# Heads with fewer gate products between them, and a down projection in 512-column steps

## The chip, the cores and the metric

The kernel runs on one core of a Trainium2 chip (trn2). The metric is the device time of one execution in microseconds. The kernel before takes 2524.01 us (median of three runs, 2521.85 to 2524.84).

Engines, as the profile names them: PE is TensorE's matrix multiply and PEld its weight load, DVE is VectorE, ACT is ScalarE, POOL is GpSimd, SP is SyncE, which issues the transfers.

## The reference

Two layers over 512 latent tokens and 256 context tokens of width 1024. Each layer has three token mixers side by side (retention, grouped-query attention, mLSTM), a gated merge, an output projection, and a gated MLP of width 2816 with a convolution of three taps; each sub-layer ends in a layer norm. In the last layer only latent tokens are asked for.

```
pl = split_proj(modulate(x, shift, scale) @ w_in + b_in)        # queries, keys, values, three gates
y_a = softmax(q @ k.T / 8) @ v                                  # 8 heads, 2 key/value groups, keys: context and latents
z = sigmoid(g_r) * (y_r @ w_r) + sigmoid(g_a) * (y_a @ w_a) + sigmoid(g_m) * (y_m @ w_m)
x = layer_norm(alpha * x + gate * (z @ w_out), ln1_g, ln1_b)
u = conv3(modulate(x, ...) @ w_up) + conv_b;   a, g = split(u)
x = layer_norm(alpha * x + gate * ((silu(g) * a) @ w_down), ln2_g, ln2_b)
```

Everything is float32. The kernel forms a product of float32 matrices from three products of a shorter float type: each operand is split into a high and a low part (`h`, `l`), and high x high, low x high and high x low are added up in PSUM.

## The kernel before

Tokens lie in tiles of 128 (`t` 0 to 3 latents, 4 and 5 context). Weights stream in blocks of 512 KB: a transfer into `raw` (five buffers), ACT casts the high part `wh`, DVE subtracts the low part `wl` (two buffers each; `wblock`, lines 308 to 315).

A Python scheduler, `Mixer`, writes PE's order at build time; the orders of the other engines come from the framework. Its foreground is the list of big products. Background generators (mLSTM, retention, attention, layer norms) are stepped between them: after a step, a generator that yields `d` isn't stepped again until foreground and background products worth `d` of the Mixer's own microseconds have been written (`step_bg`). A foreground that needs a background result steps the generators by force until the result is there (`run`).

Attention (`attention`, generator) takes one head of one query tile per step. Step n writes the scores of head n (`score`, tile `psc`: 2 products of 512 columns, 2 of 256, then maximum, exponential, sum, scaling on DVE and ACT), the six transposes of head n-2 (`flip`, tile `pPT`), and after every fourth head the value products (`av`, tile `pAV`). Then it yields 3.5 (line 1018). PSUM has two pools: three banks "g" for big products, five banks "p" for all the rest; `pAV` keeps one of the five for eight heads.

In layer 1 the foreground beside attention is, in this order: 24 gate blocks (24 products of 512 columns each; `fm`, a chance for the background after every 6), the branch products of mLSTM and retention (`merge(0)`, `merge(1)`), those of attention for tiles 0 and 1 (`merge(2)`, needs both tiles), the output projection of tiles 0 and 1, then both again for tiles 2 and 3. When tiles 0 and 1 are through the output projection their layer norm starts as background (`finish`): sums and scaling on DVE and ACT give `xn`, which PE transposes (`ptr`) for the MLP. Before that, one modulation product (`pp`, `pm`) goes through PE. `gate_rows` spreads the gate of the sub-layer over the partitions (`pgr`).

The MLP works in four groups of the hidden width (5, 5, 6 and 6 blocks of 128). Each group is projected up (`fm`), convolved, multiplied with its gate, split into `ah` and `al`, and projected down (`tm`, line 463): the activation tile is the stationary operand, 256 columns of `w_down` move. The first weight block of a quarter `q` of the 1024 columns holds all but the last two k of the group, the second the last two. Two tiles share a bank. When it is complete, `accumulate` (lines 1109 to 1125) multiplies it by the gate row and adds it to X, two operations on DVE. The fourth group of each layer also feeds the layer norm; it isn't touched by the change.

Of the kernel before, what the change touches and what calls it, by code (L numbers as in the profile page):

```python
# [13 lines left out]
OP = mybir.AluOpType  # L14
# [5 lines left out]
DEPTH = 2  # L20
# [4 lines left out]
NF = D_FF // 128  # L25
# [68 lines left out]
def layout(inputs):  # L94
    f = {k: np.asarray(v) for k, v in inputs.items()}
    A = {}
    A["x"] = f["x"].reshape(SEQ, D)
    A["ctx"] = f["ctx"].reshape(CTX, D)
    A["cT"] = np.stack([f["c"].reshape(8, 128).T, f["c_ctx"].reshape(8, 128).T], axis=2)
    w = f["w_mod"].reshape(DEPTH, 2, 4, 128, 24, 256)  # L100
    A["wmod"] = w.transpose(0, 4, 1, 3, 2, 5).reshape(DEPTH, 24, 2, 128, 1024)
    A["bmodT"] = f["b_mod"].reshape(DEPTH, 6, 8, 128).transpose(0, 3, 1, 2).reshape(DEPTH, 128, 48)
    w_in, b_in = f["w_in"], f["b_in"]
    glb = np.zeros((DEPTH, 128), np.float32)
    for dst, src in ((0, O_LI), (32, O_LI + 4), (64, O_LF), (96, O_LF + 4)):
        glb[:, dst:dst + 4] = b_in[:, src:src + 4]
    fm = [w_in[:, :, c:c + 128] for c in FM_COLS]
    A["wfm"] = np.stack([b.reshape(DEPTH, 8, 128, 128).transpose(0, 2, 1, 3).reshape(DEPTH, 128, 1024) for b in fm], 1)
    A["bfm"] = np.stack([glb] + [b_in[:, c:c + 128] for c in FM_COLS], 2)
    A["wtm"] = np.stack([w_in[:, :, c:c + 256].reshape(DEPTH, 2, 4, 128, 256).transpose(0, 1, 3, 2, 4)  # L110
                         .reshape(DEPTH, 2, 128, 1024) for c in TM_COLS], 1)
    vg = np.concatenate([w_in[:, :, TM_COLS[1]:TM_COLS[1] + 256], w_in[:, :, O_LI:O_LI + 16]], 2)
    A["wvg"] = vg.reshape(DEPTH, 8, 128, 272).transpose(0, 2, 1, 3).reshape(DEPTH, 128, 2176)
    A["btm"] = np.stack([b_in[:, c:c + 256] for c in TM_COLS], 1)
    w = np.stack([f["w_br_mlstm"], f["w_br_ret"], f["w_br_att"]], 1).reshape(DEPTH, 3, 4, 128, 4, 256)
    A["wbr"] = w.transpose(0, 1, 4, 3, 2, 5).reshape(DEPTH, 3, 4, 128, 1024)
    w = f["w_out"].reshape(DEPTH, 2, 4, 128, 4, 256)
    A["wout"] = w.transpose(0, 4, 1, 3, 2, 5).reshape(DEPTH, 4, 2, 128, 1024)
    w = f["w_up"].reshape(DEPTH, 8, 128, 2 * NF, 128)
    A["wup"] = w.transpose(0, 3, 2, 1, 4).reshape(DEPTH, 2 * NF, 128, 1024)  # L120
    w = f["w_down"].reshape(DEPTH, NF, 128, 4, 256)
    A["wdn"] = w.transpose(0, 3, 2, 1, 4)
    A["convT"] = np.stack([f["conv_w"][:, i].reshape(DEPTH, 2 * NF, 128).transpose(0, 2, 1) for i in range(3)]
                          + [f["conv_b"].reshape(DEPTH, 2 * NF, 128).transpose(0, 2, 1)], 3).reshape(DEPTH, 128, 8 * NF)
    A["gnT"] = np.concatenate([f["mlstm_gn_g"].reshape(DEPTH, 4, 128).transpose(0, 2, 1),
                               f["ret_gn_g"].reshape(DEPTH, 4, 128).transpose(0, 2, 1)], 2)
    A["qkg"] = np.concatenate([f["attn_qn_g"], f["attn_kn_g"]], 1)
    dl = f["ret_decay_logit"]
    t = np.zeros((DEPTH, 128, 16), np.float32)
    for d in range(2):  # L130
        for j in range(2):
            t[:, :64, 2 * d + j] = dl[:, d, 2 * j, None]
            t[:, 64:, 2 * d + j] = dl[:, d, 2 * j + 1, None]
        for h in range(4):
            t[:, :, 4 + 4 * d + h] = dl[:, d, h, None]
            t[:, 64 * d:64 * d + 64, 12 + h] = dl[:, d, h, None]
    A["dlog"] = t
    for n in ("ln1_g", "ln1_b", "ln2_g", "ln2_b"):
        A[n] = f[n]
    A["cst"] = _constants()  # L140
    return {k: np.ascontiguousarray(v) for k, v in A.items()}
# [62 lines left out]
def _program(es, nc, tc, I, OUT):  # L204
# [258 lines left out]
    def tm(srcs, lhs, tiles, nks, evac, hook=None, w=256):  # L463
        per = 512 // w
        banks = [tiles[i:i + per] for i in range(0, len(tiles), per)]
        gs = [None] * len(banks)
        tot = sum(nks)
        done = 0
        for src, nk in zip(srcs, nks):
            h, l = src() if callable(src) else wblock(src, nk * w)  # L470
            for bi, ts in enumerate(banks):
                if hook:
                    yield from hook(int(done > 0), ts)
                if done == 0:
                    gs[bi] = gt()
                for i, t in enumerate(ts):
                    for k, pi in [(k, pi) for k in range(nk) for pi in (0, 1)] + [(k, 2) for k in range(nk)]:
                        mm(gs[bi][:, w * i:w * i + w], lhs(done + k, t, pi == 1), (l if pi == 2 else h)[:, w * k:w * k + w],
                           start=(done + k == 0 and pi == 0 and i == 0),
                           stop=(done + k == tot - 1 and pi == 2), skip_group_check=True)  # L480
                    yield
                if done + nk == tot:
                    evac(ts, gs[bi][:, :w * len(ts)].rearrange("p (t c) -> p t c", c=w))
            done += nk

    def x_lhs(xh, xl):
# [359 lines left out]
    def attention(l, qtiles, ydir):  # L846
# [137 lines left out]
        for n in range(len(units) + 3):  # L984
# [28 lines left out]
            if n < len(units) and units[n][1] == 7 and units[n][0] != qtiles[-1]:  # L1013
                yield 2.0
                Q[tn] = stack(qn)
                yield 2.0
            else:
                yield 3.5 if n < len(units) and units[n][0] < 4 else 2.8
        M.done.add(f"a{l}")

    def brow(l, i):
# [87 lines left out]
    def accumulate(l, X, xslot, ts, g, q, rows, first, final):  # L1109
        hf, co = divmod(q, 2)  # L1110
        i = 0
        while i < len(ts):
            n = 1
            while i + n < len(ts) and (ts[i + n] >= 4) == (ts[i] >= 4):
                n += 1
            t = ts[i]
            tmp = stg()
            t3 = tmp[:, :256 * n].rearrange("p (t c) -> p t c", c=256)
            V.tensor_tensor(t3, g[:, i:i + n], bc(rows[int(t >= 4)][hf][:, 256 * co:256 * co + 256], 1, n), op=OP.mult)
            xs = X[:, xslot(t):xslot(t) + n, 256 * q:256 * q + 256]  # L1120
            V.scalar_tensor_tensor(xs, xs, ALPHA if first else 1.0, t3, op0=OP.mult, op1=OP.add)
            if final:
                for u in range(t, t + n):
                    V.bn_stats(bst[:, u, 6 * q:6 * q + 6], X[:, xslot(u), 256 * q:256 * q + 256])
            i += n

    LAT, ALL = ((0, 512),), ((0, 512), (512, 768))

    def layer(l, xT, key):
# [301 lines left out]
        for gr, (go, gnum) in enumerate(zip(GOFF, GROUPS)):  # L1431
# [50 lines left out]
            def keep(q, si, src):  # L1482
# [12 lines left out]
                        kept[q, si] = h, m  # L1495
                return kept[q, si]

            for ts in (((0, 1), (2,), (3,)) if final and last else trips if final else (tuple(range(nqt)),)):
                for q in range(4):
                    n0 = gnum - 2  # L1500
# [37 lines left out]
```

## Time and profile before

| | |
|---|---|
| three runs | 2521.85, 2524.84, 2524.01 us |
| the profiled execution | 2534.83 us, span 2533.0 us, mean granted clock 0.985 |
| PE busy | 2435.9 us, 96% of the span |
| DVE busy | 1574.9 us, 62% |
| ACT busy | 1002.7 us, 40% |
| share of the chain that ended last | PE 85%, DVE 7%, DMA 4%, ACT 3% |

The profile is one execution. A product's duration in it is its way through the array, about 281 ns for 256 columns and 393 ns for 512, and neighbours overlap; the pace is read from the step from one start to the next, or from a stretch divided by its count. PEclk is the granted clock of PE: 1.00 is 2.4 GHz, 0.50 is 1.2 GHz. A number in brackets behind a row is how long the engine had been idle before it, with the instruction that ended the wait.

### The profile page before, as it was taken

The numbers are of one execution on the slowest core, as the hardware profiler recorded it, in microseconds if no ns is written. First come the engines' busy times: TensorE is split into PE (matmuls) and PEld (weight loads), VectorE is DVE, ScalarE is ACT, GpSimd is POOL, SyncE is SP. The second block draws the span as 40 slices with busy tenths as digits, with TensorE's granted clock in tenths as the row PEclk, the third lists the DMA queues.
The fourth block names the chain that finished last, engine by engine and source line by source line (L and its number), as shares of the span: only waits on it lengthen the run. The fifth ranks groups of instructions, "written<-read, shape, count | busy, mean of one in ns | idle before, by whom it ended". The sixth has DMA issues, their size and how long they took to land.

```text
span 2533.0 us, 41667 instructions
## 1 busy us (share of the span) xinstructions
PE 2435.9 (96%) x16552; PEld 2155.9 (85%) x16552; DVE 1574.9 (62%) x3308; ACT 1002.7 (40%) x1802; POOL 92.2 (4%) x111
## 2 busy tenths in 40 slices
PE   6999999999899999999999989999999989999998
PEld 4977998888788988999998878779787788988887
DVE  5556465545477885555545773767565877855557
ACT  4433321455433473232313353434254455633332
POOL 1000001000000000000000010000110000000000
PEclk9999999999999999999999999999999998999999
DMA  7253524322554562212121383354434444533232
GB/s 257 90 171 134 167 94 140 111 82 86 175 165 165 193 243 84 74 53 77 53 76 55 125 292 126 99 172 140 161 122 146 135 134 167 176 105 99 83 106 67
DMA packets 147651, 329.21 MB, mean 130 GB/s; under 512 B 15872, under 2 KB 59136, under 8 KB 147456
## 3 DMA queue, kind: packets, MB, share of 16 engines
q1 hardware_dynamic: 147456, 326.54, 39.4%
q8 instruction: 131, 2.15, 0.4%
q14 instruction: 64, 0.52, 0.1%
HBM read 283.49 MB, written 42.99 MB: 129 GB/s over the span
## 4 chain that ended last, share of the span: by engine, by line
PE 85%; DVE 7%; DMA 4%; ACT 3%; issue 1%; POOL 0%; SPq 0%; DVEq 0%; ACTq 0%; POOLq 0%
PE g L214 72%; PE pAV L214 2%; PE psc L214 2%; PE pPT L218 2%; DVE wl L314 2%; DMA raw<-in_wmod_dram 1%; PE pE L214 1%; PE pNf L214 1%; ACT wh L313 1%; PE pp L214 1%; PE pU L214 1%; DMA raw<-in_wtm_dram 1%; PE pO L214 1%; DMA raw<-in_wup_dram 1%; PE pyt L218 0%
## 5 line engine op out<-in xcount | busy, mean ns | idle before, releaser
L214 PE MATMUL g<-xh,wh 128*128 128x512 f32 (+1 forms) x2448 | 827.9, 353 | 11.0 <-ACT xh L1315 4.7
L214 PE MATMUL g<-xl,wh 128*128 128x512 f32 (+1 forms) x2448 | 814.8, 348 | 1.4 <-DVE xl L442 0.8
L314 DVE TENSOR_TENSOR wl<-raw,wh 128x1024 fp32r<-128x1024 f32 (+3 forms) x358 | 411.9, 1151 | 354.5 <-ACT wh L313 270.8
L313 ACT CAST wh<-raw 128x1024 fp32r<-128x1024 f32 (+3 forms) x358 | 355.2, 992 | 644.4 <-PE g L214 575.5
L214 PEld LDWEIGHTS g<-xh,wh 128*128 128x128 f32 x2448 | 466.7, 191 | 80.2 <-issue 10.0
L214 PEld LDWEIGHTS g<-xl,wh 128*128 128x128 f32 x2448 | 468.0, 191 | 57.3 <-DVE xl L1316 1.3
L214 PE MATMUL g<-xh,wl 128*128 128x512 f32 (+1 forms) x2448 | 511.1, 348 | 3.0 <-DVE wl L314 3.0
L214 PEld LDWEIGHTS g<-xh,wl 128*128 128x128 f32 x2448 | 402.4, 191 | 61.1 <-DVE wl L314 3.4
L214 PE MATMUL g<-wh,ah 128*128 128x256 f32 x808 | 207.3, 284 | 3.6 <-ACT ah L1459 3.6
L214 PE MATMUL g<-wh,al 128*128 128x256 f32 x808 | 206.5, 283 | 2.7 <-DVE al L1460 2.7
L214 PE MATMUL g<-wh,xh 128*128 128x256 f32 (+1 forms) x768 | 203.4, 295 | 3.1 <-ACT wh L313 1.7
L214 PE MATMUL g<-wh,xl 128*128 128x256 f32 (+1 forms) x768 | 199.1, 290 | 3.4 <-DVE xl L1377 2.1
L214 PEld LDWEIGHTS g<-wh,ah 128*128 128x128 f32 x808 | 153.9, 190 | 4.9 <-ACT ah L1459 4.2
L214 PEld LDWEIGHTS g<-wh,xh 128*128 128x128 f32 x768 | 150.9, 196 | 8.2 <-issue 3.3
L214 PEld LDWEIGHTS g<-wh,al 128*128 128x128 f32 x808 | 153.9, 190 | 4.1 <-DVE al L1460 3.5
L214 PEld LDWEIGHTS g<-wh,xl 128*128 128x128 f32 x768 | 151.1, 197 | 4.2 <-DVE xl L1377 2.4
L1420 ACT ACTIVATE tc<-g,conv 128x512 f32<-128x512 f32 (+1 forms) x142 | 96.8, 682 | 132.8 <-PE g L214 131.6
L214 PE MATMUL g<-wl,ah 128*128 128x256 f32 x808 | 144.9, 283 | 0.8 <-DVE wl L314 0.8
L1421 DVE SCALAR_TENSOR_TENSOR tc<-g,conv,tc 128x511 f32<-128x511 f32 (+1 forms) x142 | 88.7, 625 | 83.8 <-ACT tc L1420 83.1
L414 POOL TENSOR_TENSOR rstd<-veps,mhalf 128x1 f32<-128x1 f32 (+3 forms) x68 | 71.8, 1057 | 1797.6 <-DVE veps L412 1783.2
L947 ACT ACTIVATE Pe<-psc,mx 128x256 f32<-128x256 f32 (+1 forms) x144 | 80.7, 565 | 142.2 <-DVE mx L942 96.7
L214 PE MATMUL g<-wl,xh 128*128 128x256 f32 (+1 forms) x768 | 129.1, 289 | 0.9 <-DVE wl L314 0.8
(279 smaller groups left out, 3159.0 us busy)
## 6 DMA issues: line engine op xcount, KB each, us to landing
raw<-in_wup_dram SPq DMA_DIRECT2D x108, 512.0 KB, 3.5
raw<-in_wmod_dram SPq DMA_DIRECT2D x96, 512.0 KB, 5.4
raw<-in_wfm_dram SPq DMA_DIRECT2D x80, 512.0 KB, 3.6
raw<-in_wtm_dram SPq DMA_DIRECT2D x32, 512.0 KB, 5.3
raw<-in_wout_dram SPq DMA_DIRECT2D x32, 512.0 KB, 3.6
raw<-in_wbr_dram SPq DMA_DIRECT2D x28, 512.0 KB, 4.3
dr_g<-stg SPq DMA_DIRECT2D x48, 256.0 KB, 2.0
raw<-in_wdn_dram SPq DMA_DIRECT2D x20, 512.0 KB, 3.6
```

Source lines behind the costliest of these rows:

```text
L214: nc.tensor.matmul(out, lhsT, rhs, **kw)
L218: nc.tensor.transpose(out, in_, ident)
L313: S.copy(h[:, :n], raw[:, :n])
L314: V.tensor_tensor(l[:, :n], raw[:, :n], h[:, :n].bitcast(F32), op=OP.subtract)
L414: G.tensor_tensor(r, t, mhalf[:, :n], op=OP.pow)
L947: S.activation(pe[:, a:b], prs[si][:, :b - a], AF.Exp, bias=mx[:, 3:4], scale=0.125, accum_out=sm[:, si:si + 1])
L1420: S.activation(t[:, a:b], g, AF.Identity, bias=conv[:, jj, 3:4], scale=conv[:, jj, 1:2])
L1421: V.scalar_tensor_tensor(t[:, a + 1:b], g[:, :b - a - 1], conv[:, jj, 0:1], t[:, a + 1:b], op0=OP.mult, op1=OP.add)
```

## The change

Two edits.

In layer 1's attention the generator yields 2.6 in place of 3.5 after each of the first 16 steps (the heads of the first two query tiles). With PE's chances of 6 products of 512 columns, that is 12 gate products between two heads in place of 18.

The down projection of the first three groups of each layer goes through a new function, `tm_wide`: 512 columns of `w_down` move per product, for two halves `hf` of the width in place of four quarters. Each tile has a bank of its own, alternately from pool "g" and pool "p" (there named `gx`). Weight blocks hold two k of 512 columns (one k in the last block of a group of 5): 6 blocks per group in place of 8, from a second arrangement of the same weights. `accumulate_wide` does for one tile and 512 columns what `accumulate` did for two tiles and 256.

```
+    w = f["w_down"].reshape(DEPTH, NF, 128, 2, 512)
+    A["wdw"] = w.transpose(0, 3, 2, 1, 4)
...
+    def tm_wide(srcs, lhs, tiles, nks, evac):
+        gs = {}
+        tot = sum(nks)
+        done = 0
+        for src, nk in zip(srcs, nks):
+            h, l = wblock(src, nk * 512)
+            for i, t in enumerate(tiles):
+                if done == 0:
+                    gs[t] = gt() if i % 2 == 0 else pt("gx")
+                for k, pi in [(k, pi) for k in range(nk) for pi in (0, 1)] + [(k, 2) for k in range(nk)]:
+                    mm(gs[t], lhs(done + k, t, pi == 1), (l if pi == 2 else h)[:, 512 * k:512 * k + 512],
+                       start=(done + k == 0 and pi == 0), stop=(done + k == tot - 1 and pi == 2))
+                yield
+                if done + nk == tot:
+                    evac(t, gs.pop(t))
+            done += nk
...
-                yield 3.5 if n < len(units) and units[n][0] < 4 else 2.8
+                yield 2.6 if l == DEPTH - 1 and n < 16 else 3.5 if n < len(units) and units[n][0] < 4 else 2.8
...
+    def accumulate_wide(X, xslot, t, g, hf, rows, first):
+        tmp = stg()[:, :512]
+        V.tensor_tensor(tmp, g, rows[int(t >= 4)][hf], op=OP.mult)
+        xs = X[:, xslot(t), 512 * hf:512 * hf + 512]
+        V.scalar_tensor_tensor(xs, xs, ALPHA if first else 1.0, tmp, op0=OP.mult, op1=OP.add)
...
+            if not final:
+                for hf in range(2):
+                    srcs = [I["wdw"][l, hf][:, k:min(k + 2, go + gnum)].rearrange("p k c -> p (k c)")
+                            for k in range(go, go + gnum, 2)]
+                    yield from tm_wide(srcs, alh, range(nqt), [s.shape[1] // 512 for s in srcs],
+                                       lambda t, g: accumulate_wide(X, xslot, t, g, hf, rows, gr == 0))
+                continue
```

PE's order is the same before and after but for the six down projections and the stretch of layer 1's attention. Three places. (In the changed kernel the lines of the helpers are shifted by 2, those further down by more.)

PE, the first down projection of layer 0, before: one tile of the first block.

```order
L214 MATMUL g<-wh,ah 128x256
L214 MATMUL g<-wh,al 128x256
L214 MATMUL g<-wh,ah 128x256
L214 MATMUL g<-wh,al 128x256
L214 MATMUL g<-wh,ah 128x256
L214 MATMUL g<-wh,al 128x256
L214 MATMUL g<-wl,ah 128x256 x3
```

The same place now: two tiles of the first block.

```order
L216 MATMUL g<-wh,ah 128x512
L216 MATMUL g<-wh,al 128x512
L216 MATMUL g<-wh,ah 128x512
L216 MATMUL g<-wh,al 128x512
L216 MATMUL g<-wl,ah 128x512 x2
L216 MATMUL gx<-wh,ah 128x512
L216 MATMUL gx<-wh,al 128x512
L216 MATMUL gx<-wh,ah 128x512
L216 MATMUL gx<-wh,al 128x512
L216 MATMUL gx<-wl,ah 128x512 x2
```

Nine products of 256 columns per tile and block became six of 512, and neighbouring tiles write to different pools. Of 1920 products 960 are left.

PE, the end of layer 1's attention, before (`psc` scores, `pPT` transposes, `pAV` value products; `g<-xh,wh` is already the attention branch of tiles 2 and 3).

```order
L214 MATMUL psc<-KH,Qo 128x512
L214 MATMUL psc<-KL,Qo 128x512
L214 MATMUL psc<-KH,Qo 128x256
L214 MATMUL psc<-KL,Qo 128x256
L218 MATMUL pPT<-ident,Pe 128x128 x18
L214 MATMUL pAV<-PT,va 64x128 x24
L214 MATMUL g<-xh,wh 128x256
L214 MATMUL g<-xl,wh 128x256
```

Now the last head's transposes stand 36 products apart, with the output projection of tiles 0 and 1 (`g<-wh,xh`) between them, and 60 more of its products follow the value products; the last piece reads:

```order
L216 MATMUL g<-wh,xh 128x256
L216 MATMUL g<-wh,xl 128x256
L216 MATMUL g<-wl,xh 128x256 x4
L216 MATMUL pAV<-PT,va 64x128 x24
L216 MATMUL g<-wh,xh 128x256
L216 MATMUL g<-wh,xl 128x256
```

The transposes of tile 0's normalised rows stood behind all 96 products of that branch and ahead of the output projection; before:

```order
L214 MATMUL g<-xh,wl 128x256 x4
L214 MATMUL pm<-selm,part 128x8 x2
L214 MATMUL pp<-raw,silc 32x256 x8
L218 MATMUL ptr<-ident,xn 128x128 x8
L214 MATMUL g<-wh,xh 128x256
L214 MATMUL g<-wh,xl 128x256
```

Now they stand within it, behind 66 of its products:

```order
L216 MATMUL g<-xh,wh 128x256
L216 MATMUL g<-xl,wh 128x256
L216 MATMUL pm<-selm,part 128x8 x2
L216 MATMUL pp<-raw,silc 32x256 x8
L220 MATMUL ptr<-ident,xn 128x128 x8
L216 MATMUL g<-xh,wh 128x256
L216 MATMUL g<-xl,wh 128x256
L216 MATMUL g<-xh,wl 128x256 x4
```

Elsewhere in that stretch: the first branch product stood behind the scores of the thirteenth head, the transposes of the eleventh and 12 gate products; now it stands right behind the scores of the eighteenth and the transposes of the sixteenth, since fewer gate products went between the heads before. The two gate-row products (`pgr`) stood right ahead of a head's scores and right behind its transposes; now they stand 6 and 18 products behind a head's transposes.

DVE, the layer norm of tile 0 in layer 1 (`mv`, `veps`, `lnrow`, `lnsum`, `nm`), before.

```order
L1124 BN_STATS bst<-z 128x6 x2
L1082 BN_AGGR mv<-bst 128x2
L412 TENSOR_SCALAR veps<-mv 128x1
L1086 SCALAR_TENSOR_TENSOR z<-z,mv,lnrow 128x512 x2
L950 TENSOR_TENSOR sme<-sme 128x1
L1087 SCALAR_TENSOR_TENSOR z,lnsum<-z,rstd,lnrow 128x512 x2
L951 RECIPROCAL sme<-sme 128x1
L1093 TENSOR_SCALAR nm<-lnsum 128x1
```

Now (lines 1392, 1393 and 1402 are the branch's evacuations and the split of z, line 316 is the low half of a weight block):

```order
L1101 BN_AGGR mv<-bst 128x2
L316 TENSOR_TENSOR wl<-raw,wh 128x1024
L1393 TENSOR_TENSOR z<-z,stg 128x256
L414 TENSOR_SCALAR veps<-mv 128x1
L1105 SCALAR_TENSOR_TENSOR z<-z,mv,lnrow 128x512 x2
L1402 SCALAR_TENSOR_TENSOR xl<-z,xh 128x256
L1392 SCALAR_TENSOR_TENSOR stg<-stg,g 128x256 x2
L316 TENSOR_TENSOR wl<-raw,wh 128x1024
L1402 SCALAR_TENSOR_TENSOR xl<-z,xh 128x256
L1106 SCALAR_TENSOR_TENSOR z,lnsum<-z,rstd,lnrow 128x512 x2
L1393 TENSOR_TENSOR z<-z,stg 128x256 x2
```

What stood between small softmax operations now stands between branch evacuations and weight splits; from the projection's last evacuation to the mean `nm` there are eleven operations of the branch and three weight splits, where there was one weight split and the last head's score maxima.

## Rows read from the trace of the kernel before

**Rows 1.** The page: engines; the chain that ended last.

```profile
PE 2435.9 (96%) x16552; PEld 2155.9 (85%) x16552; DVE 1574.9 (62%) x3308; ACT 1002.7 (40%) x1802; POOL 92.2 (4%) x111
...
PE 85%; DVE 7%; DMA 4%; ACT 3%; issue 1%; POOL 0%; SPq 0%; DVEq 0%; ACTq 0%; POOLq 0%
```

**Rows 2.** Windows (us; busy and count by engine; PEclk, DMA): six downs, one up.

```profile
989.70:1032.75 43.05, 43.05 (x362) 42.81 (x361) 23.15 (x33) 7.85 (x12) 0.00 (x0) 1.00 0.34 106
1116.15:1158.45 42.30, 42.30 (x362) 42.30 (x361) 23.15 (x33) 7.67 (x10) 0.00 (x0) 1.00 0.27 85
1258.55:1309.55 51.00, 51.00 (x434) 51.00 (x433) 23.44 (x33) 8.31 (x11) 0.22 (x1) 1.00 0.23 73
2206.90:2236.65 29.75, 29.11 (x242) 28.55 (x241) 17.81 (x31) 8.18 (x15) 0.00 (x0) 1.00 0.47 151
2291.10:2323.00 31.90, 30.36 (x241) 29.95 (x240) 17.91 (x25) 7.35 (x11) 0.00 (x0) 0.95 0.33 104
2388.30:2422.40 34.10, 34.10 (x289) 34.06 (x288) 18.50 (x26) 8.09 (x10) 0.00 (x0) 1.00 0.32 101
2323.00:2388.30 65.30, 65.30 (x290) 54.12 (x289) 38.51 (x47) 27.56 (x34) 0.00 (x0) 1.00 0.30 93
```

**Rows 3.** Windows: five heads of layer 1 among gate products.

```profile
1865.98:1892.72 26.74, 26.74 (x135) 22.60 (x135) 18.50 (x41) 15.03 (x37) 1.64 (x1) 1.00 0.36 119
```

**Rows 4.** Timeline, PE (start, us, what, [idle before, releaser]): first branch products.

```profile
1939.38 0.51 PE L214 MATMUL g<-xh,wh 128*128 128x512 f32 x1 [1.77 <-ACT xh L1315]
...
1944.75 0.80 PE L214 MATMUL g<-xh,wh 128*128 128x512 f32 x1 [2.95 <-ACT xh L1315]
```

**Rows 5.** Windows: the lowered clock there.

```profile
1939.95:1950.19 10.24, 7.09 (x19) 5.21 (x20) 3.53 (x8) 2.19 (x5) 0.00 (x0) 0.50 0.62 195
```

**Rows 6.** Timeline, PE: a gate-row product.

```profile
2027.31 1.13 PE L214 MATMUL pgr<-dg,ones 128*128 128x512 f32 x2 [1.86 <-ACT Pe L947]
```

**Rows 7.** Timeline, PE: after the last head's scores.

```profile
2078.57 0.89 PE L218 MATMUL pPT<-ident,Pe 128*128 128x128 f32 x6 [3.02 <-ACT Pe L947]
2082.38 1.51 PE L218 MATMUL pPT<-ident,Pe 128*128 128x128 f32 x6 [2.91 <-DVE Pe L955]
...
2088.74 0.39 PE L214 MATMUL g<-xh,wh 128*128 128x256 f32 x1 [0.69 <-ACT xh L1321]
```

**Rows 8.** Timeline, PE: output projection of tiles 2 and 3, last wait.

```profile
2111.39 0.58 PE L214 MATMUL g<-wh,xl 128*128 128x256 f32 x1 [1.52 <-DVE xl L1377]
```

**Rows 9.** Timeline, PE: layer 1's second down projection.

```profile
2296.60 0.39 PE L214 MATMUL g<-wh,ah 128*128 128x256 f32 x1 [0.85 <-ACT ah L1459]
```

**Rows 10.** Timeline, DVE and ACT: around the layer norm of tile 0.

```profile
2074.23 0.69 DVE L1119 TENSOR_TENSOR stg<-g,grow 128x512 f32<-128x512 f32 x1 [1.01 <-PE g L214]
...
2084.45 1.52 ACT L1102 ACTIVATE xn<-z,nb,rstd 128x512 f32<-128x512 f32 x2
...
2091.08 0.42 DVE L1367 SCALAR_TENSOR_TENSOR stg<-stg,g 128x256 f32<-128x256 f32 x1 [1.67 <-PE g L214]
...
2093.32 1.22 DVE L314 TENSOR_TENSOR wl<-raw,wh 128x1024 fp32r<-128x1024 f32 x1
```

**Rows 11.** Timeline, PE and ACT: scores and second exponentials of two heads.

```profile
1870.84 0.40 PE L214 MATMUL psc<-KH,Qe 128*128 128x512 f32 x1
...
1875.03 0.48 ACT L947 ACTIVATE Pe<-psc,mx 128x256 f32<-128x256 f32 x1
...
1876.31 0.40 PE L214 MATMUL psc<-KH,Qo 128*128 128x512 f32 x1
...
1879.02 0.46 ACT L947 ACTIVATE Pe<-psc,mx 128x256 f32<-128x256 f32 x1
...
1881.78 0.39 PE L214 MATMUL psc<-KH,Qe 128*128 128x512 f32 x1
```

**Rows 12.** Windows: from tiles 0 and 1's output projection to past rows 8.

```profile
2074.00:2111.80 37.80, 27.44 (x229) 24.70 (x228) 29.32 (x73) 21.37 (x43) 3.04 (x4) 0.89 0.43 141
```

**Rows 13.** Chain, in order of time: value products of four heads.

```profile
2041.25 2.77 PE pAV L214 x48
```

## Prediction

> **What bounds the kernel now.** I read the page first: TensorE (PE) is busy 96% of the span and makes 85% of the chain that ended last [rows 1]. So time is won in two ways only: the same products in less PE time, or fewer moments in which PE waits. Next I cut the stretches that the change touches out of the windows view, to see whether PE is at its own pace there. In the six down projections of the groups that change it mostly is: PE is busy for all of four of them, and falls short by 0.6 and 1.5 us in two of layer 1 [rows 2]. In layer 1's attention I went through the timeline for gaps. While the gate products lie between the heads there are none: five heads in a row, PE busy 26.74 of 26.74 us, VectorE (DVE) 18.50, ScalarE (ACT) 15.03 [rows 3]. The gaps come later: where the branch products begin [rows 4, 5], at the gate-row products [rows 6], at the last heads [rows 7], and where the output projection of tiles 2 and 3 begins [rows 8].
>
> **The down projection.** Six stretches of 43.05, 42.30, 51.00, 29.75, 31.90 and 34.10 us make 232.1 us [rows 2] for 360, 360, 432, 240, 240 and 288 products of 256 columns, 1920 in all. The longest gives 51.00/432 = 118.1 ns per product; at that pace the six would take 226.7 us, so 5.4 us are waits. Nearly all of those are in layer 1: 29.75 against 240 x 0.1181 = 28.3, and 31.90 against 28.3. The second is seen as waits on the last gated activation, one of 0.85 us on its high part, with a PEclk of 0.95 over the stretch [rows 2, 9].
>
> After the change there are 960 products of 512 columns. The trace has their price: an up-projection group of layer 1, 288 products of 512 columns, each with a stationary tile of its own as here, takes 65.30 us, 226.7 ns each [rows 2]. 960 x 0.2267 = 217.6 us: 9.1 us less by pace, 9.5 ns for each pair of products.
>
> The waits: before, the first block holds all but the last two k of a group, so PE asks for these after one block, for a group of 5 after 4 tiles x 9 products, 4.3 us. Now blocks hold two k each; PE asks for the fourth k after 4 x 6 x 0.2267 = 5.4 us and for the fifth after 10.9. The waits on activations should go: up to 5.4 us.
>
> What is new: per half of the columns all tiles of a group are open at once (six PSUM banks in layer 0, four in layer 1), and they close together in the last block. For a group of 5 that block is a single k: 3 products per tile, 0.68 us, while DVE needs two operations of about 0.69 us per tile [rows 10]. So DVE falls behind by up to 6 x 0.7 = 4.2 us in layer 0. PE doesn't see it if the next half finds free banks: its first tile takes the third bank of the "g" pool, or one emptied long before, and each later tile comes 6 x 0.2267 = 1.36 us after the one before, which DVE's 1.38 just holds. The low half of the next weight block is wanted only after four products (0.9 us) and stands between the evacuations in DVE's order. I leave 1 us for such waits, and take 13.5 us for this part. Ends: 8 (pace alone, 1 us of it lost) to 14.5.
>
> A rule speaks for less. The Trainium skill, "TensorE: Matmul & The Clock Gate", section "Back-to-back issue gap", puts the step between products at the columns over the clock plus 2.5 ns, so that half as many products would save 2.5 ns per pair, by that estimate 960 x 2.5 = 2.4 us. This trace differs: 118.1 and 226.7 ns for the two sizes [rows 2], a fixed part of some 9.5 ns, and the measurement decides.
>
> **The heads.** No product is added; the order changes. A head is 4 score products and 6 transposes, and for every four heads 24 pairs of value products follow. In the first 16 heads 12 gate products stand between two heads, not 18. PE's step from score to score is 5.47 us now (1881.78 - 1876.31 [rows 11]), of which 18 x 0.2267 = 4.08 are gates; with 12 it is 1.39 + 2.72 = 4.1. The next head's score writes the banks that this head's exponentials read (five banks, one held by the value products). In a quiet head the second exponential ends 1879.48 - 1876.31 = 3.2 us after the score began; in a crowded one, with query work of the next tile on DVE, 1875.51 - 1870.84 = 4.7 us [rows 11]. So quiet heads pass, and crowded ones make PE wait up to 0.6 us. In the new order of DVE and ACT the weight casts, transposed copies and gate activations fall behind the exponentials. I put 2 us on all of it; ends 0 and 14 x 0.6 = 8.
>
> What it brings is another meeting of waits after the gates, which I take in turn.
> - Entry of the branch products. The gates end at 1939.38 - 1.77 = 1937.6; then PE waits for copies of y, last until 1944.75, 7.1 us on [rows 4]. Those loads wait for buffers, whatever PE does. Now a head (1.4 us) stands in between, so the wait shrinks by 1.4. Then the clock: for 10.24 us it is granted at 0.50 (1.2 GHz), with 7.09 us of work in it [rows 5], worth some 3 us. Whether it still falls is open: I take 2 us gain, ends 0 and 4.4.
> - Gate-row products: PE waits 1.86 us for an exponential to free a bank [rows 6]. They still stand close behind a head. 1 us gain, ends -1 and 4.
> - The last heads. Three times six transposes and the value products stand in a row with nothing between; PE waits 3.02, 2.91 and 0.69 us [rows 7]. Now 36 products of the output projection (4.3 us) stand between. These waits go. But what is late next is the layer norm of tile 0. It can begin when the output projection of tiles 0 and 1 has ended, at 2074.0, and its rows were ready at 2084.45 + 1.52 = 2085.97, 11.9 us later, in the shadow of just those waits [rows 10]. PE wanted them only after 96 branch products. Now the branch products begin at once, the transposes of those rows (ptr) stand after 66 of them (7.8 us) and ten small modulation products (I put 1 us), and DVE has the branch evacuations mixed into the norm: eleven operations of 0.42 and two more weight splits of 1.22, less some 1.0 of score maxima, 6.0 us more [rows 10]. So the rows are ready at 17.9 us, PE asks at 9 to 10.5, and waits 7 to 8 us where no wait was.
>   The sum: before, 37.80 us from that point to past the last wait at 2111.39 [rows 8, 12], of which 5.2 are the last head's work (value products 2.77 [rows 13], four scores, 18 transposes). After: 17.9; then 1.1 for eight transposes, 3.5 for the last 30 branch products, 3.8 for the first 32 of the next projection, and 2 of waiting there for DVE, which empties the last three branch products behind tile 1's norm: 28.3. A lowered clock after the long wait adds 2. 37.8 - 5.2 - 30.3 = 2 us gain, ends -4 and 9.
>
> The heads together: -2 + 2 + 1 + 2 = 3 us gain. The whole: 13.5 + 3 = 16.5 us. The profiled execution took 2534.83 us (span 2533.0), 10.8 above the median of 2524.01; from the one the sum leads to 2518.3, from the other to 2507.5. The forecast is for the median: 2508.
>
> **Rivals.**
> - A, the heads pay in full: 2500. The norm is ready soon after PE asks, as DVE gets through its branch work early (wait 2 instead of 7 us, gain 7), and the clock stays up at the branch entry (gain 4): 13.5 - 1 + 4 + 1 + 7 = 24.5. For it: DVE is busy only 29.32 of 37.80 us in that stretch [rows 12]. Against: the order puts three weight splits and eleven branch operations ahead of the norm's mean.
> - B, the heads give back: 2517. Crowded heads cost 6 us and the norm's wait is 4 longer than computed: 13.5 - 6 - 2 + 1.5 = 7. For it: 18.50/5 = 3.7 us of DVE work per head [rows 3] against a step of 4.1.
> - C, slower than before: 2532. One mechanism: PE waits at every score for the exponentials of the head before, because DVE and ACT, working through their orders, fall behind a step of 4.1 us. It decides from 4.1 + 16.5/14 = 5.3 us between score and exponential on; at 5.6 us it is 14 x 1.5 = 21 against 13.5. Against it: even the crowded head among the gates takes 4.7, and a step with fewer gate products brings fewer casts and evacuations.
> - D, the wide products don't keep the pace of the up projection, with 2.4 us of pace left in place of 9.1: 2514. Against it: both sizes stand in [rows 2]. The skill's formula above would bring this.
>
> **How the numbers follow.** Forecast 0.62 (its own range 2502 to 2514), A 0.15, B 0.13, C 0.05, D 0.05. The known ends are 8 to 14.5 for the down projection and -13 to 17 for the heads. The range, 2496 to 2518, leaves out C, half of B and the end of A. About 0.2% (5 us) is what a measurement of this kernel can tell from no change. Faster by more than that (below 2519): forecast, A, D and half of B, 0.88; same 0.07, the other half of B; slower 0.05, C.
>
> **What the profile after would show.** The six down stretches together near 219 us, those of layer 1 near 27.5, 27.5 and 33, with no wait on the activation. Between two of the first 16 heads a step near 4.1 us and waits of PE on exponentials below 0.6. No gap between the last transposes; a new one of 5 to 9 us ahead of ptr, until xn. I am wrong if the down stretches together stay above 224 us, if ptr doesn't wait, or if the first 16 heads lose over 6 us.

## The result and the profile after

The changed kernel takes 2514.66 us (median of 7 runs, 2510.74 to 2519.7); the kernel before, run beside it, 2526.43 (7 runs, 2521.85 to 2532.82). The ratio is 0.995, 95% interval 0.9933 to 0.9967: 11.8 us less, 8.3 to 16.9. Forecast were 2508 us, in a range of 2496 to 2518, and 16.5 us of gain. Times are medians, and of all runs below one, of 6521.38 us in the kernel with 2.6 for 32 heads, is left out.

The two profiled executions are 24 us apart (spans of 2533.0 and 2509.0 us). About a third of that arises in stretches that are the same in both programs (the first down projection starts 7 us earlier), so below only the changed stretches are compared. The page after, engines and chain, against [rows 1]:

```profile
PE 2417.0 (96%) x15592; PEld 2093.9 (83%) x15592; DVE 1571.2 (63%) x3296; ACT 1003.1 (40%) x1791; POOL 94.7 (4%) x111
...
PE 85%; DVE 6%; DMA 4%; ACT 3%; issue 1%; SPq 0%; POOL 0%; DVEq 0%; ACTq 0%; POOLq 0%
```

960 matmuls fewer, 19 us less of busy PE, the other engines as before. The windows view of the six down projections and the same up projection, against [rows 2] (busy and count of PE, PEld, DVE, ACT, POOL; PEclk; DMA share; GB/s):

```profile
982.70:1024.85 42.15, 42.15 (x183) 33.95 (x181) 18.05 (x26) 6.85 (x10) 0.00 (x0) 1.00 0.27 84
1108.25:1150.11 41.86, 41.86 (x183) 33.80 (x181) 18.27 (x26) 6.86 (x10) 0.00 (x0) 1.00 0.19 66
1250.16:1300.33 50.17, 50.17 (x219) 40.56 (x217) 23.31 (x31) 7.97 (x10) 0.72 (x1) 1.00 0.19 63
2189.67:2217.93 28.26, 28.26 (x123) 22.70 (x122) 14.59 (x28) 7.28 (x13) 0.00 (x0) 1.00 0.41 138
2272.34:2300.05 27.71, 27.71 (x122) 22.52 (x121) 14.47 (x20) 6.47 (x9) 0.00 (x0) 1.00 0.29 96
2365.35:2398.75 33.40, 33.40 (x146) 27.03 (x145) 18.13 (x23) 7.57 (x9) 0.00 (x0) 1.00 0.29 95
2300.05:2365.35 65.30, 65.30 (x290) 54.07 (x288) 40.74 (x51) 28.01 (x34) 0.00 (x0) 1.00 0.34 105
```

The six make 223.5 us, where 232.1 were and 219 were forecast. PE is busy in all of every stretch and the clock is full: the waits on the activations are gone. But the pace isn't the up projection's: 50.17/216 = 232 ns per product against 65.30/288 = 226.7, in the same trace.

From layer 1's first score to the first up product, the windows view after:

```profile
1850.06:2119.20 269.14, 249.67 (x1775) 219.09 (x1773) 196.68 (x416) 142.46 (x310) 10.05 (x7) 0.97 0.45 145
```

The same stretch before, with the same 1775 products:

```profile
1861.20:2137.40 276.20, 254.61 (x1775) 223.98 (x1773) 195.45 (x416) 141.28 (x309) 7.96 (x7) 0.95 0.44 140
```

Of the 7.1 us that it is shorter, only 2.1 are idle time of PE (276.20 - 254.61 = 21.6 before, 19.5 now). The other 4.9 are busy time for the same products, and PEclk rose from 0.95 to 0.97. Before, the clock stood at 0.50 four times in this stretch, 27.3 us in all: [rows 5] and these three,

```profile
2028.69:2032.11 3.42, 3.42 (x18) 3.42 (x18) 1.42 (x4) 1.83 (x3) 0.00 (x0) 0.50 0.27 101
2079.89:2086.72 6.83, 4.34 (x34) 4.04 (x36) 5.00 (x18) 4.50 (x10) 1.48 (x2) 0.50 0.06 20
2110.61:2117.44 6.83, 6.05 (x28) 6.05 (x29) 2.74 (x5) 1.28 (x2) 0.00 (x0) 0.50 0.27 79
```

now twice, 13.7 us in all:

```profile
1942.80:1949.63 6.83, 4.77 (x10) 3.05 (x11) 2.68 (x5) 1.40 (x3) 0.00 (x0) 0.50 0.47 146
2082.75:2089.58 6.83, 4.87 (x23) 4.88 (x24) 6.08 (x18) 4.39 (x9) 1.70 (x2) 0.50 0.22 80
```

PE was busy for 20.9 us of the four and for 9.6 of the two. If half of that is lost at half the clock, an estimate, 10.5 us were lost before and 4.8 are now.

Within the stretch, the timeline of PE after shows the four places of the forecast. The scores of three heads among the gates (start, us, what):

```profile
1866.04 0.39 PE L216 MATMUL psc<-KH,Qe 128*128 128x512 f32 x1
...
1870.13 0.39 PE L216 MATMUL psc<-KH,Qo 128*128 128x512 f32 x1
...
1874.22 0.39 PE L216 MATMUL psc<-KH,Qe 128*128 128x512 f32 x1
```

The step is 4.09 us (5.47 in [rows 11]), without a gap. Then the rows with a wait, a selection: the branch entry, against [rows 4], a new wait of a later head for its queries, and the place behind the last head, where the last transposes and value products now have no idle time ahead of them (3.02, 2.91 and 0.69 us in [rows 7]):

```profile
1938.46 0.49 PE L216 MATMUL g<-xh,wh 128*128 128x512 f32 x1 [0.50 <-ACT xh L1340]
...
1940.00 0.50 PE L216 MATMUL g<-xl,wh 128*128 128x512 f32 x1 [1.04 <-DVE xl L1341]
...
1944.86 0.80 PE L216 MATMUL g<-xh,wh 128*128 128x512 f32 x1 [3.65 <-ACT xh L1340]
...
1995.75 0.41 PE L220 MATMUL pPT<-ident,Pe 128*128 128x128 f32 x2 [1.94 <-DVE Qo L943]
...
2076.32 0.39 PE L216 MATMUL g<-xh,wh 128*128 128x256 f32 x1 [1.64 <-DVE stg L1392]
...
2084.71 1.97 PE L220 MATMUL ptr<-ident,xn 128*128 128x128 f32 x8 [6.06 <-ACT xn L1121]
...
2095.83 0.39 PE L216 MATMUL g<-wh,xl 128*128 128x256 f32 x1 [0.44 <-DVE xl L1402]
```

The new wait ahead of `ptr` is there: 6.06 us, ended by `xn` on ACT. The windows view from the last output product of tiles 0 and 1 to that point, and to the first up product:

```profile
2067.10:2119.20 52.10, 42.18 (x342) 40.01 (x340) 43.57 (x92) 26.63 (x45) 5.14 (x4) 0.93 0.54 179
2067.10:2084.71 17.61, 9.91 (x89) 8.92 (x87) 15.03 (x41) 7.04 (x14) 2.20 (x3) 0.94 0.70 236
```

PE began with these rows 17.6 us after the output projection, and DVE was busy for 15.03 of them. ACT had both halves of them ready at 2083.84 + 1.52 = 2085.36, after 18.3 us (17.9 forecast):

```profile
2083.84 1.52 ACT L1121 ACTIVATE xn<-z,nb,rstd 128x512 f32<-128x512 f32 x2 [1.17 <-DVE nb L1119]
```

### The profile page after: what moved, and what is told of

Read it like the earlier page. It is cut to its first block, busy times and chain, and to the rows that moved or that the text cites. A ratio compares the mean times of both kernels' runs of the same rounds, so it can differ in the third digit from the quotient of the medians.

```text
span 2509.0 us, 39685 instructions
## 1 busy us (share of the span) xinstructions
PE 2417.0 (96%) x15592; PEld 2093.9 (83%) x15592; DVE 1571.2 (63%) x3296; ACT 1003.1 (40%) x1791; POOL 94.7 (4%) x111
## 4 chain that ended last, share of the span: by engine, by line
PE 85%; DVE 6%; DMA 4%; ACT 3%; issue 1%; SPq 0%; POOL 0%; DVEq 0%; ACTq 0%; POOLq 0%
PE g L216 68%; PE gx L216 4%; PE pAV L216 2%; PE psc L216 2%; PE pPT L220 2%; DVE wl L316 2%; DMA raw<-in_wtm_dram 1%; PE pE L216 1%; PE pNf L216 1%; ACT wh L315 1%; DMA raw<-in_wmod_dram 1%; PE pU L216 1%; PE pp L216 1%; PE pO L216 1%; DMA raw<-in_wup_dram 1%
## 5 line engine op out<-in xcount | busy, mean ns | idle before, releaser
L1446 DVE SCALAR_TENSOR_TENSOR tc<-g,conv,tc 128x511 f32<-128x511 f32 (+1 forms) x142 | 88.7, 625 | 76.7 <-ACT tc L1445 76.5
L216 PE MATMUL g<-wh,ah 128*128 128x256 f32 (+1 forms) x328 | 106.5, 340 | 2.7 <-ACT ah L1484 2.7
L216 PEld LDWEIGHTS g<-wl,xh 128*128 128x128 f32 x768 | 107.6, 193 | 1.5 <-DVE wl L316 1.5
L216 PE MATMUL g<-wh,al 128*128 128x256 f32 (+1 forms) x328 | 105.5, 337 | 1.4 <-DVE al L1485 1.4
L957 DVE TENSOR_REDUCE mx<-psc 128x1 f32<-128x256 f32 (+1 forms) x144 | 72.2, 537 | 38.7 <-PE psc L216 38.4
L1447 DVE SCALAR_TENSOR_TENSOR tc<-g,conv,tc 128x511 f32<-128x511 f32 (+1 forms) x142 | 88.9, 627 | 4.2
```

Source lines behind the costliest of these rows:

```text
L216: nc.tensor.matmul(out, lhsT, rhs, **kw)
L957: V.tensor_reduce(mx[:, si:si + 1], pr[:, :b - a], axis=mybir.AxisListType.X, op=OP.max)
L1446: V.scalar_tensor_tensor(t[:, a + 1:b], g[:, :b - a - 1], conv[:, jj, 0:1], t[:, a + 1:b], op0=OP.mult, op1=OP.add)
L1447: V.scalar_tensor_tensor(t[:, a:b - 1], g[:, 1:b - a], conv[:, jj, 2:3], t[:, a:b - 1], op0=OP.mult, op1=OP.add)
```

## The experiments

Theory: the two parts add, the down projection gains less than forecast because its products step at 232 ns, and the heads gain more. Open were where the 232 ns come from, and whether the wait ahead of `ptr` is a loss.

### Each part alone

The changed kernel with 3.5 in place of 2.6, and the kernel before with 2.6:

```
-                yield 2.6 if l == DEPTH - 1 and n < 16 else 3.5 if n < len(units) and units[n][0] < 4 else 2.8
+                yield 3.5 if n < len(units) and units[n][0] < 4 else 2.8
```

> The wide down projection alone, with the heads as before (3.5). Theory: the two parts add. The changed kernel's profile gives the six down stretches 223.5 us for 232.1, so this kernel gains 8.6 us on the median of before, and its heads, from layer 1's first score to the first up product, take 276 us as before. Rival: the down part is worth the 13.5 us of the forecast, and the heads lose 2. Rival: the down part is worth under 4 us in time, because what it saves is waited for at the next group's first products. In the profile a step of 232 ns again in all six stretches.

> The heads at 2.6 alone, with the down projection of before. Theory: 7 us gain, as between the two profiles from layer 1's first score to the first up product (276.2 to 269.2 us): 2 lost among the gates, 1 won at the branch entry, 2 in the branch stretch, 6 to 8 behind the last head; the down stretches near 232 as before. Rival, the forecast's size: 3 us, with the rest of the 7 being chance between two executions; then this profile shows 273 us. Rival: no gain in time, since the norm's wait ahead of ptr (6.1 us in the changed kernel) gives it all back.

Measured: the down projection alone 2518.22 us, ratio 0.9963 (0.9949 to 0.9977), 9.3 us gained; the heads alone 2519.56 us, ratio 0.9969 (0.9958 to 0.998), 7.9 us gained, both against 2527.48. The windows view of the kernel with the down projection alone, its last down stretch and the heads' stretch:

```profile
2368.77:2402.16 33.39, 33.39 (x145) 27.03 (x144) 18.12 (x23) 7.56 (x9) 0.00 (x0) 1.00 0.29 95
...
1849.80:2124.10 274.30, 252.57 (x1776) 221.74 (x1774) 195.74 (x416) 141.41 (x309) 7.85 (x7) 0.96 0.44 140
```

and of the kernel with the heads alone, layer 1's second down stretch and the heads' stretch:

```profile
2276.04:2306.43 30.39, 28.85 (x241) 28.44 (x240) 17.91 (x25) 7.37 (x11) 0.00 (x0) 1.00 0.35 109
...
1855.40:2123.30 267.90, 250.11 (x1775) 219.45 (x1773) 196.57 (x416) 142.41 (x310) 8.25 (x7) 0.97 0.46 146
```

The heads' stretch is 276.2 and 274.3 us with the old order, 269.1 and 267.9 with the new one; the down stretches follow the other edit. 9.3 + 7.9 = 17.2 us is more than the 11.8 of both, and just above the upper end of its interval (8.3 to 16.9); the two carry intervals of their own (5.8 to 12.9 and 5.1 to 10.6). So these measurements show no departure from a plain sum, but they leave room for one of several microseconds. In the profiles the down stretches are the same with and without the heads' edit, but for one: the second of layer 1, in the old form, takes 30.39 us here at a PEclk of 1.00, and 31.90 at 0.95 in [rows 2], with the same 1.54 us of idle PE. The 1.5 us between them are a lowered clock that only one of the two executions has.

### What sets 232 ns

The changed kernel's trace gave a hint: within one down stretch the products of one stationary slice took nearly the same step each time, in 191 of 310 cases to two nanoseconds, while all steps lie between 224 and 243 but for the first of each layer. The tiles `ah` and `al` are 774 columns wide and 3104 bytes apart, so their slices start at different places modulo 512 bytes; the moving blocks always start at the same one (128 modulo 512), and in the up projection both operands do. In layer 1 the 512 tokens leave room to shift the start within the tile:

```
-                        ah.append(St("ah", F32R))
-                        al.append(St("al", F32R))
+                        oh, ol = COL[j] if last else (0, 0)
+                        ah.append(St("ah", F32R)[:, oh:])
+                        al.append(St("al", F32R)[:, ol:])
```

`COL` holds the columns by which a tile has to be shifted. In layer 0 the order of products and of banks was changed.

> What sets 232 ns per wide product where the up projection has 226.7? Five of the six down stretches are changed in one way each. Layer 0: group 1 as in the changed kernel; group 2 takes the three products of a k in the order high x high, then low weights x high, then high weights x low, so that two in a row share their stationary tile; group 3 gives tiles 0 to 2 banks of pool g and 3 to 5 banks of pool p, in place of alternating. Layer 1: the tiles ah and al start at a column that puts every stationary slice of group 1 at the same address modulo 512 bytes as the moving blocks, of group 2 at one address modulo 512 that is 96 bytes from that of the moving blocks, group 3 unchanged, and the narrow group 4 as group 1. Theory (addresses; the 774-column tiles lie 3104 bytes apart, so that the slices of neighbouring tiles differ modulo 512, and the same addresses gave the same step within 1 ns): steps of 227 ns in layer 1's group 1, and in group 2 as well if only the change of address matters, 232 if the distance does; about 232 in the other four; in the narrow group 4 a step of 120 in place of 118. Rival (order of products): 227 in layer 0's group 2 alone. Rival (banks): 227 in layer 0's group 3 alone. Rival (a moving weight block is slower than a moving activation): 232 everywhere.

The windows view: layer 0's groups 2 and 3, layer 1's groups 1 to 3.

```profile
1112.23:1153.82 41.59, 41.59 (x183) 33.80 (x182) 18.26 (x26) 6.83 (x9) 0.00 (x0) 1.00 0.22 67
1253.89:1303.96 50.07, 50.07 (x219) 40.54 (x217) 23.30 (x31) 7.96 (x10) 0.70 (x1) 1.00 0.19 63
2196.83:2224.46 27.63, 27.63 (x122) 22.70 (x121) 14.54 (x28) 7.27 (x13) 0.00 (x0) 1.00 0.42 141
2278.86:2306.97 28.11, 28.11 (x121) 22.60 (x120) 14.47 (x20) 6.46 (x9) 0.00 (x0) 1.00 0.28 94
2372.28:2405.61 33.33, 33.33 (x146) 27.03 (x144) 18.14 (x23) 7.55 (x9) 0.00 (x0) 1.00 0.28 95
```

With equal addresses the median step is 227 ns, and 28.26 us became 27.63 (its first five steps are 633, behind the gate-row products, 236, 228, 233 and 231; then every step is 226 or 227). With a constant distance of 96 bytes it is 234: so the distance counts, and not only its change. The pair order and the bank order gave 231.1 and 231.8 ns on average, against 232.5 and 232.2: both rivals fall, and so does the slow weight block. The narrow fourth group, aligned, went from a median of 118 to 120 ns, as expected. Layer 0's untouched group 1 kept 231.9 ns. Two more kernels tried other distances in groups 1 to 3.

> Which distance between the address of the stationary slice and that of the moving block (modulo 512 bytes) costs how much? Layer 1's groups 1, 2 and 3 have 32, 64 and 128 bytes for every product; known are 0 (227 ns) and 96 (234). Theory (any distance but 0 is slow): 232 to 235 in all three. Rival (multiples of 64 are free): 232 to 235, 227, 227. Rival (multiples of 128): slow, slow, 227. Whether the address alone is changed shows in layer 0, which stays at 232.

> As e6, with distances of 256, 16 and 320 bytes. Theory (any distance but 0 is slow): 230 to 236 in all three. Rival (multiples of 64): 227, slow, 227. Rival (multiples of 128 or 256): 227, slow, slow.

The windows view for 32, 64 and 128 bytes, and then for 256, 16 and 320:

```profile
2190.68:2219.07 28.39, 28.39 (x122) 22.70 (x121) 14.60 (x28) 7.26 (x13) 0.00 (x0) 1.00 0.40 137
2273.48:2301.47 27.99, 27.99 (x121) 22.56 (x120) 14.46 (x20) 6.46 (x9) 0.00 (x0) 1.00 0.28 95
2366.79:2400.26 33.47, 33.47 (x145) 27.13 (x144) 18.13 (x23) 7.54 (x9) 0.00 (x0) 1.00 0.28 94
```

```profile
2199.25:2226.88 27.63, 27.63 (x123) 22.69 (x122) 14.55 (x28) 7.28 (x13) 0.00 (x0) 1.00 0.41 141
2281.28:2308.48 27.20, 27.20 (x122) 22.52 (x121) 14.41 (x20) 6.46 (x9) 0.00 (x0) 1.00 0.28 97
2373.76:2407.35 33.59, 33.59 (x145) 27.07 (x144) 18.14 (x23) 7.56 (x9) 0.00 (x0) 1.00 0.28 94
```

Mean steps of 233.3, 233.3 and 232.4 ns for 32, 64 and 128 bytes, of 226.8, 226.7 and 233.3 for 256, 16 and 320; layer 0 stays at 231.9, 232.5 and 232.2 in both. The three kernels of this section ran once each, at 2519.50, 2512.24 and 2520.88 us; only their steps are read here. No theory had this right: 256 and 16 are as good as 0, while 32, 64, 96, 128 and 320 (64 beyond 256) are slow. It fits a pattern that repeats every 256 bytes; how wide its good part is beyond 16 bytes, and what in the chip makes it, these runs don't show. Two limits: all moving blocks start at 128 modulo 512 bytes, so the runs can't tell the distance from the stationary slice's own address, since only that was shifted. And they show it for whole stretches at one distance. In the mixed streams of the changed kernel a product's own distance doesn't tell its step: those at distance 0 took 228 to 237 ns there, 232 on average.

### Is the wait ahead of ptr a loss?

```
-            yield 7.0
+            yield 11.0 if l == DEPTH - 1 and t == tiles[0] else 7.0
```

> The changed kernel, with the first normalised rows' transposes (ptr) asked for 42 products later: behind the last 30 branch products and 12 of the output projection of tiles 2 and 3 (4.9 us of PE work at 0.12 us each). Theory (the wait is PE's loss): PE fills the 6.1 us wait with those products, so the stretch from the last output product of tiles 0 and 1 to the first up product (52.1 us in the changed kernel) falls to 48, and ptr waits 1 to 1.5 us. Rival (DVE is what is late there: busy 25.6 of 28.9 us): the wait moves into the output projection and to the up projection's entry; the stretch stays at 51 to 53. In time 0 to 4 us below the changed kernel, so 12 to 16 below before by the first, 10 to 13 by the second.

The timeline of PE around `ptr`, rows with a wait:

```profile
2089.78 0.46 PE L216 MATMUL g<-xh,wh 128*128 128x256 f32 x1 [1.64 <-DVE stg L1392]
...
2096.62 0.36 PE L216 MATMUL g<-wh,xh 128*128 128x256 f32 x1 [0.77 <-ACT wh L315]
...
2101.32 1.36 PE L220 MATMUL ptr<-ident,xn 128*128 128x128 f32 x8 [1.68 <-ACT xn L1121]
...
2105.20 0.39 PE L216 MATMUL g<-wh,xl 128*128 128x256 f32 x1 [0.25 <-DVE xl L1402]
```

The windows view from the last output product to the first up product:

```profile
2079.86:2128.60 48.74, 42.05 (x342) 39.29 (x340) 42.97 (x92) 26.52 (x45) 2.99 (x4) 0.96 0.59 192
```

The wait falls to 1.68 us and the stretch to 48.7 us: 3.4 us less, of which 3.2 are idle time of PE (52.10 - 42.18 = 9.9 to 6.7), so the wait doesn't come back behind. The theory holds in the profile. In time the kernel stands at 2515.81 us, ratio 0.9951 (0.9937 to 0.9965), no different from the changed kernel; 3.4 us lie within those intervals.

With this edit and aligned addresses in layer 1's three groups together:

> The changed kernel with the late rows' transposes (as in e4) and, in layer 1, every stationary slice of ah and al of groups 1 to 3 at the moving blocks' address modulo 512. Theory: steps of 227 ns, stretches of 27.6, 27.2 and 32.7 us in place of 28.26, 27.71 and 33.40 (1.9 us), and 49 us for 52 from the last output product of tiles 0 and 1 to the first up product (3.4 us): 5 us below the changed kernel, 17 below before. Rival: time that another engine gives back in the up projections behind: the stretches shrink and the time stays 12 below before.

```profile
2190.30:2217.93 27.63, 27.63 (x123) 22.70 (x121) 14.66 (x28) 7.27 (x13) 0.00 (x0) 1.00 0.43 141
2272.33:2299.53 27.20, 27.20 (x122) 22.53 (x120) 14.41 (x20) 6.47 (x9) 0.00 (x0) 1.00 0.28 97
2364.81:2397.45 32.64, 32.64 (x146) 27.04 (x144) 18.10 (x23) 7.57 (x9) 0.00 (x0) 1.00 0.28 97
2073.30:2122.00 48.70, 40.83 (x343) 37.87 (x341) 42.98 (x92) 26.55 (x45) 2.98 (x4) 1.00 0.60 195
```

The windows view shows all four stretches at their forecast, and the time is 2511.61 us against 2528.96, ratio 0.9925 (0.9911 to 0.9939): 17.4 us gained. That is the best kernel here; its lead on the changed kernel is 5.3 us by the stretches (1.3 of them busy time at a higher clock, 1.00 for 0.93), and the two intervals just overlap, so in time it is not shown.

### How close may the heads stand?

The yield in line 1037 of the changed kernel once more: 1.3 for 2.6, and 2.6 for all 32 heads (`n < 32`).

> The changed kernel with 1.3 for 2.6: 6 gate products between two of the first 16 heads in place of 12. PE's own step becomes 1.39 + 6 x 0.2267 = 2.75 us, while the exponentials of a quiet head end 3.1 to 3.4 us after its score began and DVE has some 3.7 us of work per head. Theory (exponentials and DVE set a floor for the step): PE waits at the scores, the steps settle at 3.4 to 3.8 us, and the 16 heads lose 8 to 16 us, so 5 to 12 us slower than the changed kernel. Rival: fewer gate products bring fewer casts to DVE and ACT too, the step keeps near 3 us, and the loss stays under 4 us, so within 3 us of the changed kernel.

> The changed kernel with 2.6 for all 32 heads of layer 1, so that the heads of tiles 2 and 3 that stand among the gates have 12 products between them too. Theory: no further gain; those heads had 18 products and no waits, and the losses lie at the branch entry (9.8 us) and behind the last head (18 us), which wait for copies of y and for DVE: within 3 us of the changed kernel. Rival: what won 7 us for 16 heads wins some more: 2 to 5 us faster, with the stretch from layer 1's first score to the first up product under 266 us (269.2 in the changed kernel).

With six gates between two heads: 2535.61 us, ratio 1.0033 (1.002 to 1.0046), 8.5 us slower than before, so some 20 slower than the changed kernel. The windows view of the first 16 scores and of the whole stretch, then PE's waits in the first:

```profile
1849.63:1910.27 60.64, 52.89 (x331) 43.48 (x330) 40.34 (x103) 34.22 (x89) 3.27 (x2) 0.94 0.24 79
1849.63:2139.16 289.53, 260.14 (x1776) 225.79 (x1774) 196.75 (x416) 143.89 (x311) 10.04 (x7) 0.94 0.42 136
```

```profile
1857.99 0.44 PE L220 MATMUL pPT<-ident,Pe 128*128 128x128 f32 x2 [2.88 <-ACT Pe L966]
...
1888.75 0.50 PE L216 MATMUL psc<-KH,Qo 128*128 128x512 f32 x1 [1.33 <-ACT Pe L966]
...
1891.95 0.87 PE L220 MATMUL pPT<-ident,Pe 128*128 128x128 f32 x6 [2.22 <-ACT PT L983]
```

The theory holds in kind: the first 16 heads wait for exponentials, at transposes as well as at scores, and PE idles for 7.8 us there. Its size was short; the whole stretch grows by 20 us. Half of that is idle time (289.53 - 260.14 = 29.4 us against 19.5), and the other half is that nearly the same products (1776 for 1775) keep PE busy 10.5 us longer (260.14 for 249.67), at a PEclk of 0.94 for 0.97. The 32 heads at 2.6 gave 2517.2 us (median of four runs), ratio 0.9955 (0.9934 to 0.9976), a stretch of 273.9 us: nothing more is won there.

## Why the prediction was right or wrong

- The down projection, 13.5 us forecast, 8.6 in the profile, 9.3 in time alone. The waits went as told: 5.4 us before, 223.5 - 960 x 0.232 = 0.8 left, where 1 was allowed. That 0.8 is the first step in each layer, 0.4 us too long behind the gate-row products. But the 5.4 weren't all waits: 1.5 were the lowered clock of the one stretch that the kernel with the heads alone has at full clock. Against that kernel's six stretches, 230.7 us, the change wins 7 and not 8.6. The step that failed is "960 x 0.2267 = 217.6 us: 9.1 us less by pace". Measured: 960 x 0.232 = 222.7 us, 4 us less. With 223.5 us the stretches stayed half a microsecond below the 224 that the prediction named as a sign of being wrong. The up projection was the wrong price for it, although it has the same columns and a new stationary tile for each product: the slices of its stationary operand all lie at one good address modulo 512 bytes, those of the down projection don't.
- So rival D was right on the pace, more than the forecast: of its 2.4 us and the forecast's 9.1, 4 came. Its reason was another. By the formula of the Trainium skill ("TensorE: Matmul & The Clock Gate", section "Back-to-back issue gap"), which the section gives for a single product's gap in isolation, the step is columns over clock plus 2.5 ns. This trace differs: it was 512/2.4 = 213.3 plus 13.4 ns with good addresses and plus 19 on average with those of the change. And the total landed on D's 2514 by way of other terms.
- The first 16 heads: 2 us forecast. The steps are 4.1 us as told; the only wait over half a microsecond there is 0.62 us. Over the gates, the excess of the steps over the median step of their tile and shape, summed where positive, rose from 6.3 to 8.2 us.
- Branch entry: 2 us forecast, 1 measured by the same sum (9.3 from 1937.2 to 1952.0 before, 8.3 from 1937.9 to 1952.0 now). The prediction had the wait shrink by 1.4 us for the head in between; it didn't: 1.77 and 2.95 us in [rows 4] became 0.50, 1.04 and 3.65. What was won is the clock: it still falls to 0.50, for 6.83 us where it was 10.24 [rows 5].
- Gate rows and what lies around them: 1 forecast, 2.5 measured by the same sum (16.6 from 1952.0 to 2074.0 before, 14.1 from there to 2067.1 now). The wait of [rows 6] is gone and so is the lowered clock behind it, from 2028.69 on; a head's wait of 1.94 us for queries is new.
- The last heads and the norm: 2 forecast, more measured: the stretch up to the last wait in the output projection took 28.7 us (2067.1 to 2095.83) against 30.3, and the up projection's entry came 2.7 us closer behind it, 23.4 us (to 2119.22) for 26.1 before (2111.39 [rows 8] to 2137.44). Those 2.7 us weren't in the prediction: before, the clock stood at 0.50 there, from 2110.61 to 2117.44, and now it is full. The mechanism (`ptr` right behind the 66 products, rows ready after 17.9 us) was as told to 0.4 us; PE asked at 11.6 us and not at 9 to 10.5, so the wait was 6.1 and not 7 to 8.
- The heads together: 3 forecast, 7 in the two profiles, 7.9 in time alone. Over the runs with the old order (276.2, 274.3) and with the new (269.1, 267.9 and, with shifted addresses in the down projection, 272.0, 269.8, 271.3) the means differ by 5.2 us. The prediction added up waits and had the clock as a side term. In the two profiles 4.9 of the 7 us are busy time of PE at a higher granted clock; in the means over those seven runs it is about half, 2.5 of the 5.2.

So the time fell into the range, 6.7 us above its point. The pace of the wide products was 5 us too good and the heads were 2 to 4 us too poor; that these nearly cancel (8.6 + 7.1 = 15.7 us in the profiles for 16.5) is luck. Of the 6.7 us, 2.4 are the kernel before, whose median beside the changed one was 2526.43 and not 2524.01; the rest is within the interval of the gain.

## What to carry to other kernels

A pace taken from another stretch of the same trace held only where the operands' addresses lay alike: compare the spread of the steps (226 and 227 there but for the first three and the last, 224 to 243 here) before using it as a price. A wait of PE that has independent products queued behind it could be filled with them even where DVE is busy nine tenths of the time (25.61 of 28.90 us): 6.1 us became 1.7. Between two heads that share banks through ACT, fewer products could stand while PE's own step (4.1 us) lay between ACT's ways for a quiet and a crowded head (3.2 and 4.7 us); a step of 2.75 us cost 20 us, and the limit between the two wasn't measured. And a gain in a stretch with waits should be split into idle time and busy time of PE: the second shows what the granted clock gave back.

## What the runs showed of the hardware

- In stretches with one constant distance (modulo 512 bytes) between the addresses of stationary slice and moving block, products of four-byte operands and 512 columns step at 226.7 to 226.8 ns for 0, 16 and 256 bytes and at 232 to 234 for 32, 64, 96, 128 and 320, at a PEclk of 1.00 throughout. With the moving blocks always at 128, it may as well be the stationary address alone.
- For 256 columns the good distance isn't the faster one: 120 ns in the median aligned, 118 unaligned, in layer 1's fourth group. The step of 120 is 106.7 plus 13.3, the same fixed part as for 512 columns.
- A run of products with good addresses reached its steady step after four or five steps behind other products: 236, 228, 233, 231, then 226 or 227, in the aligned down projection as in the up projection.
- The same 1775 products kept PE busy for 254.61 us with 27.3 us at a granted clock of 0.50, and for 249.67 us with 13.7 us at it.
